# Four of seven products of the mixer's sets with high and low parts side by side

## The chip, the cores and the metric

One core of a Trainium2 chip runs one launch of the kernel. The metric is the device time in microseconds (us), the median of the runs shown. All times below are in us unless ns is said.

## The reference, cut to what matters

The block is two gated feed-forward networks (FFNs) with a mixer between them; everything is float32, with 512 tokens and a width of 1024.

```python
x = x + 0.5 * swiglu(rmsnorm(x, g1), w_gu1, w_down1)      # 1024 -> 2 x 2816 -> 1024
h = rmsnorm(x, gm)
z = h @ w_in                                              # 1024 -> 8208 columns
cb, cc, cu, q, k, v, g_lr, r, ga, gb = split(z)
y_conv = (cb * causal_short_conv(cc * cu, conv_w)) @ w_out_conv
o = gla_chunked(q, k, v, log_a)                           # gated linear attention, 4 heads, chunks of 64
y_gla = (norm(o) * silu(r)) @ w_out_gla
x = x + (sigmoid(ga) * y_conv + sigmoid(gb) * y_gla) @ w_o
x = x + 0.5 * swiglu(rmsnorm(x, g2), w_gu2, w_down2)
return rmsnorm(x, gf)
```

## The kernel before, in words

**Products.** TensorE multiplies in fp32r. To keep float32's precision each operand is split in two: a high part (the value rounded to fp32r) and a low part (the rest). A product is then three passes: high weights on high data, high weights on low data, low weights on high data. ScalarE makes a weight's high part (`wh`, line 346), VectorE its low part (`wl`, line 347); three buffers of each exist, and `Weights.issue` makes the parts of step n+2 when step n is taken.

**Sets.** Most large matrices are multiplied in *sets*: a 2 by 2 grid of blocks is multiplied with seven block products in place of eight (Winograd's form of Strassen's scheme). The seven are called m1, p2, q6, p5, q7, p4, p3. One block product takes 512 rows of the matrix and 256 of its columns (in two halves e = 0, 1 of 128) on 256 tokens, so a pass is 4 k-blocks times 2 halves = 8 matmuls. The products share accumulators: "b" is written by m1, q6, q7 and p4, one on top of the other; "c" by p5 and then p3; "a" by p2. So after m1, q6 and q7 the state of "b" has to be copied out before the next of them may be written, and the quarters of the result are made from these copies with sums: p2's quarter is a + m1; q7's, made after q7 from p5's c, is -c - (copy at q7); p3's is c + (copy at q6); p4's is -b. Sets are numbered 0 to 11 (on `w_in`) and 12, 13 (on `w_out_gla`). `order` fixes the order of products: q6, p5, q7 of set s, m1 of the next set t, p4 of s, p2 of t, p3 of s. The last set ends q6, p5, q7, p2, p4, p3, and the first begins m1, p2.

**Two kinds of sets.** The FFNs' up sets (`PairSet`, line 562) have tiles of two PSUM banks. For most of them (`merged`) the high and low data lie side by side (`Both`, line 537: 256 high and 256 low columns per k-block), and high weights run over both in one matmul of 512 columns: left half of the tile is weights on high data, right half weights on low data; the low weights then add on the left half. That is 8 matmuls of 512 and 8 of 256. Left and right are added later by ScalarE and VectorE (`taken`, `onto`, `whole`). The mixer's sets (`Set`, line 494) use one bank per accumulator and 24 matmuls of 256 columns a product (line 517): 12 sets on `w_in` (`MSETS`: ga, gb, ga, conv, gb, conv, conv, conv, cb, cb, r, r) and 2 on `w_out_gla`. From the second set on a set is `forked`: after m1 ScalarE copies bank b into bank a (line 522), and p2 accumulates on that copy; after q6 and q7 ScalarE copies bank b to an SBUF tile of the pool `tp` (line 525).

**Around the sets.** `run_sets` (line 762) runs the products in order and calls hooks between them: the attention's steps (`gates`, `decays`, `scale`, `scores`, `state`, `output`, `squares`) for the four heads are hung on products of the first nine sets. `conv_done`, `cb_done`, `gate_done`, `r_done` and `gla_done` use the quarters: products with each other and a three-tap convolution (`convolve`, lines 1393 to 1396), gates stored to DRAM from the ScalarE queue (line 1481), silu, or the final sum (line 1600). Statements further down, such as the split of the convolution's result (`split_pair`, lines 1513 and 1514), get their place in each engine's queue from the compiler's own schedule, so they can run between products. After the `w_out_gla` sets the product with `w_o` starts with a group of four accumulators (`mm_group`, line 395).

**PSUM.** There are 8 banks. `banks` opens either six single banks (pool `mm`) and two more (pool `aux`, used by hooks and norms), or, for the up sets, four pairs with the names w, x, y, z. The pools lie one behind another in the order in which they are opened; a newly opened `mm` pool hands out its places in the order 0, 5, 4, 3, 2, 1 (this is how the program before is laid out), and later the place that has been free longest. The last plain product before FFN 1's up sets leaves its accumulator in bank 0, and w, the first pair, lies on banks 0 and 1.

Of the kernel before, what the change touches and what calls it, by code (L numbers as in the profile page):

```python
# [8 lines left out]
F32 = mybir.dt.float32  # L9
F32R = mybir.dt.float32r  # L10
# [169 lines left out]
def block_kernel(ctx: ExitStack, tc: tile.TileContext, xT, vecs, gf, gup, wgl, wts, out):  # L180
# [23 lines left out]
    def T(dtype=F32):  # L204
        return tile_of("tp", [P, S], dtype)

    stage = ExitStack()

    def banks(paired=False):

        stage.close()
        for n, b in (("pairs", 1),) if paired else (("mm", 6), ("aux", 2)):
            cnt[0] += 1
            pools[n] = stage.enter_context(tc.tile_pool(
                name=f"{n}{cnt[0]}", bufs=b, space=bass.MemoryType.PSUM, reuse_waits="tile"))

    banks()
    ctx.push(lambda *_: stage.close())
# [274 lines left out]

    class Set:


        def __init__(self, group_, done):
            self.group = group_
            self.done = done
            self.bank = {}  # L500
            self.v = {}

        def run(self, p):
            b = {"m1": "b", "p2": "a", "q6": "b", "p5": "c", "q7": "b", "p4": "b", "p3": "c"}[p]
            fresh = b not in self.bank
            if fresh:
                self.bank[b] = MM()
            o = self.bank[b]
            bh, bl = self.group.get(p)
            h, l = W.take()  # L510
            for j, (ww, aa) in enumerate(((h, bh), (h, bl), (l, bh))):
                for k in range(4):
                    for e in range(2):
                        s = slice(k * HW + e * P, k * HW + (e + 1) * P)
                        t = slice(k * HW, (k + 1) * HW)
                        to = o[:, e * HW : (e + 1) * HW]
                        nc.tensor.matmul(to, ww[:, s], aa[:, t],  # L517
                                         start=fresh and k == 0 and e == 0 and j == 0,
                                         stop=k == 3 and j == 2, skip_group_check=True)
            if p == "m1" and self.forked:  # L520
                self.bank["a"] = MM()
                nc.scalar.copy(self.bank["a"], o)  # L522
            elif p in ("m1", "q6", "q7"):
                v = T()
                nc.scalar.copy(v, o)
                self.v[p] = v
            self.done(self, p)

        def first(self):

            if self.forked:
                return self.bank["a"]
            t = T()
            nc.vector.tensor_tensor(out=t, in0=self.bank["a"], in1=self.v["m1"], op=ALU.add)
            return t
# [26 lines left out]
    class PairSet:  # L562
# [21 lines left out]
        def run(self, p):  # L584
# [4 lines left out]
            h, l = W.take()  # L589
            first = fresh  # L590

            def product(to, ww, aa):
                nonlocal first
                for k in range(4):
                    for e in range(2):
                        nc.tensor.matmul(to(e), ww[:, k * HW + e * P : k * HW + (e + 1) * P],  # L596
                                         aa(k), start=first and k == 0 and (self.merged or e == 0),
                                         stop=k == 3 and ww is l, skip_group_check=True)
                first = False

            if self.merged:
                product(lambda e: o[:, e], h, x_.both)
                product(lambda e: o[:, e, :HW], l, x_.high)
            else:
                half = self.flat(n)
                for ww, aa in ((h, x_.high), (h, x_.low), (l, x_.high)):
                    product(lambda e: half[:, e * HW : (e + 1) * HW], ww, aa)
# [41 lines left out]

    class Operands:  # L650
# [5 lines left out]
        def __init__(self, b, kind=None):  # L656
            self.b = b
            self.kind = kind
# [22 lines left out]
        def make(self, p):  # L681
# [6 lines left out]
            if self.kind is not None:  # L688
                self.parts[p] = self.kind(v)
                return  # L690
            h, l = (tile_of("op", [P, 1024], F32R) for _ in range(2))
            hv, lv = (t.rearrange("p (k t) -> p k t", t=HW) for t in (h, l))
            nc.scalar.copy(hv, v)
            nc.vector.tensor_tensor(out=lv, in0=v, in1=hv.bitcast(F32), op=ALU.subtract)
            self.parts[p] = (h, l)
# [4 lines left out]
    class DownOperands:  # L700
# [17 lines left out]
        def make(self, p):  # L718
# [11 lines left out]
            h, l = (tile_of("op", [P, 1024], F32R) for _ in range(2))  # L730
            hv, lv = (t.rearrange("p (k t) -> p k t", t=HW) for t in (h, l))
            nc.scalar.copy(hv, v)
            nc.vector.tensor_tensor(out=lv, in0=v, in1=hv.bitcast(F32), op=ALU.subtract)
            self.parts[p] = (h, l)
# [4 lines left out]
    def natural_set(ops, bank, done, ahead=1):  # L739

        used = {"a"}
        for at, p in enumerate(SEQ):
# [6 lines left out]
            bh, bl = ops.get(p)  # L749
            for u in range(2):  # L750
                h, l = W.take()
                for j, (ww, aa) in enumerate(((h, bh), (h, bl), (l, bh))):
                    for i in range(2):
                        k = 2 * u + i
                        for t in range(2):
                            s = slice(k * HW + t * P, k * HW + (t + 1) * P)
                            nc.tensor.matmul(o[t], aa[:, s], ww[:, i * 512 : (i + 1) * 512],  # L757
# [932 lines left out]
```

## Time and profile before

| | before |
|---|---|
| median of 3 runs | 1174.29 (1173.33 to 1174.67) |
| profiled execution: its time, its span | 1173.69, 1172.0 |
| granted TensorE clock, mean | 0.999 |
| the mixer's first 12 sets and the hooks between them | about 430 to 703 |
| the two `w_out_gla` sets | about 747 to 787 |
| FFN up sets | about 51 to 228 and 876 to 1056 |

The page gives busy time, share of the span and number of instructions of each engine, the chain of work that ended last, and the costliest groups of instructions. PE is TensorE, PEld its weight load, DVE VectorE, ACT ScalarE. Other views are the waits (who waited for whom), the timeline (instructions in order of start: start, duration, engine, line, operation, out<-in, and idle time before it in brackets), groups by line, and windows (busy time of each engine in a stretch). Ends of matmuls are modelled and overlap; the pace of TensorE is read from the starts.

### The profile page before, as it was taken

Reading aid. Unit: us, or ns where it says so; the run is one execution under the profiler, and the core shown is the slowest. Engines: PE = TensorE matmul, PEld = TensorE weight load, DVE = VectorE, ACT = ScalarE, POOL = GpSimd, SP = SyncE. Lnnn points to the kernel's source line nnn. Section 1 sums busy time; section 2 is a strip of 40 time slices with the busy share of each in tenths; the row PEclk is TensorE's granted clock in tenths of the full one; section 3 lists DMA queues with packets and bytes.
Section 4 is the critical chain, followed back from the end, with each engine's and each line's share of the span. In section 5 each row is a group of like instructions: output and inputs, shape, how many; then the busy total and the mean of one; then the engine's idle time right before and its main releaser. Section 6 shows DMA issues by size and latency. Waiting matters only on the chain.

```text
span 1172.0 us, 17786 instructions
## 1 busy us (share of the span) xinstructions
PE 1163.1 (99%) x7010; PEld 1038.9 (89%) x7010; DVE 922.0 (79%) x1125; ACT 668.5 (57%) x860; POOL 117.1 (10%) x153
## 2 busy tenths in 40 slices
PE   9999999999999999999999999999999999999997
PEld 8898888988888889999999998998889888898886
DVE  7997888996578965767697788586599788889955
ACT  6576666675335655565565476544456666666443
POOL 0010101111010111100111100000001111011100
PEclk9999999999999999999999999999999999999999
DMA  9477787778524488777687766540638777767721
GB/s 352 85 203 197 175 203 180 164 192 218 199 90 109 93 206 225 187 179 200 177 204 189 205 187 198 130 125 22 239 75 213 178 191 178 192 153 186 181 84 72
DMA packets 62596, 200.16 MB, mean 171 GB/s; under 512 B 6864, under 2 KB 13136, under 8 KB 62512
## 3 DMA queue, kind: packets, MB, share of 16 engines
q1 hardware_dynamic: 39088, 126.37, 32.4%
q0 software_dynamic: 18784, 68.17, 31.4%
q10 hardware_dynamic: 4640, 4.49, 1.1%
q8 instruction: 55, 0.90, 0.3%
q14 instruction: 29, 0.24, 0.1%
HBM read 124.55 MB, written 8.39 MB: 113 GB/s over the span
## 4 chain that ended last, share of the span: by engine, by line
PE 95%; DVE 2%; ACT 2%; issue 1%; ACTq 0%; POOL 0%; POOLq 0%
PE mm L517 22%; PE mm L757 13%; PE mm L381 9%; PE y L596 9%; PE w L596 9%; PE z L596 9%; PE mm L395 7%; PE x L596 4%; PE mm L974 4%; PE aux L757 4%; PE aux L974 1%; PE aux L1297 1%; PE aux L1278 1%; PE aux L1256 1%; DVE wl L347 0%
## 5 line engine op out<-in xcount | busy, mean ns | idle before, releaser
L346 ACT CAST wh<-f 128x1024 fp32r<-128x1024 f32 (+1 forms) x341 | 356.4, 1047 | 369.4 <-PE mm L517 86.2
L347 DVE TENSOR_TENSOR wl<-f,wh 128x1024 fp32r<-128x1024 f32 (+1 forms) x341 | 412.8, 1216 | 122.6 <-ACT wh L346 113.5
L517 PE MATMUL mm<-op,wh 128*128 128x256 f32 x1568 | 208.1, 285 | 0.4 <-ACT mm L522 0.4
L324 POOL DMA_DIRECT2D f<-f x126 | 108.6, 862 | 921.8 <-DVE wl L347 524.1
L517 PEld LDWEIGHTS mm<-op,wh 128*128 128x128 f32 x1568 | 196.9, 191 | 2.1 <-ACT mm L522 0.8
L517 PE MATMUL mm<-op,wl 128*128 128x256 f32 x784 | 110.0, 283 | 0.0
L757 PE MATMUL mm<-wh,op 128*128 128x512 f32 x432 | 106.9, 389 | 0.0
L517 PEld LDWEIGHTS mm<-op,wl 128*128 128x128 f32 x784 | 101.2, 192 | 0.1
L757 PEld LDWEIGHTS mm<-wh,op 128*128 128x128 f32 x432 | 80.9, 188 | 16.7
L381 PE MATMUL mm<-op,wh 128*128 128x512 f32 x384 | 91.0, 389 | 0.0
L381 PEld LDWEIGHTS mm<-op,wh 128*128 128x128 f32 x384 | 72.0, 188 | 15.0
L596 PE MATMUL w<-op,wh 128*128 128x512 f32 (+1 forms) x352 | 73.1, 353 | 0.5 <-DVE tp L491 0.5
L596 PE MATMUL y<-op,wh 128*128 128x512 f32 (+1 forms) x384 | 73.3, 338 | 0.0
L596 PE MATMUL z<-op,wh 128*128 128x512 f32 (+1 forms) x320 | 72.7, 371 | 0.0
L596 PEld LDWEIGHTS y<-op,wh 128*128 128x128 f32 x384 | 58.4, 190 | 6.2
L395 PE MATMUL mm<-op,wh 128*128 128x512 f32 x256 | 63.8, 391 | 0.0
L596 PEld LDWEIGHTS w<-op,wh 128*128 128x128 f32 x352 | 56.2, 190 | 8.2 <-issue 0.9
L596 PEld LDWEIGHTS z<-op,wh 128*128 128x128 f32 x320 | 54.0, 189 | 8.2
L757 PE MATMUL mm<-wl,op 128*128 128x512 f32 x216 | 57.7, 389 | 0.0
L395 PEld LDWEIGHTS mm<-op,wh 128*128 128x128 f32 x256 | 47.8, 188 | 10.3
L333 DVE TENSOR_TENSOR f<-f,f 128x1024 f32<-128x1024 f32 x42 | 51.3, 1221 | 0.8
L757 PEld LDWEIGHTS mm<-wl,op 128*128 128x128 f32 x216 | 40.5, 188 | 8.4
(313 smaller groups left out, 1690.4 us busy)
## 6 DMA issues: line engine op xcount, KB each, us to landing
f<-wts SPq DMA_DIRECT2D x219, 512.0 KB, 4.5
f<-f POOLq DMA_DIRECT2D x126, 512.0 KB, 5.0
X<-xT SPq DMA_DIRECT2D x8, 256.0 KB, 5.3
xs<-X POOLq DMA_DIRECT2D x8, 256.0 KB, 2.4
ga<-tp ACTq DMA_DIRECT2D x8, 256.0 KB, 3.2
gb<-tp ACTq DMA_DIRECT2D x8, 256.0 KB, 3.7
tp<-ga SPq DMA_DIRECT2D x8, 256.0 KB, 4.2
y<-tp SPq DMA_DIRECT2D x7, 256.0 KB, 2.3
```

The costliest lines, as they stand in the source:

```text
L324: return nc.gpsimd.dma_start(out_, a, accum_op=ALU.add).ins
L333: nc.vector.tensor_tensor(out=s3, in0=a11, in1=a21, op=ALU.add)
L346: self.cast = nc.scalar.copy(h[:, :w], raw[:, :w]).ins
L347: nc.vector.tensor_tensor(out=l[:, :w], in0=raw[:, :w], in1=h[:, :w].bitcast(F32), op=ALU.subtract)
L381: nc.tensor.matmul(o, w[:, i * P : (i + 1) * P], a[k], start=j == k == 0, stop=j == 2 and k == kt - 1)
L395: nc.tensor.matmul(o[c], w[:, s : s + P], a[k], start=k == 0 and j == 0, stop=k == kt - 1 and j == 2)
L517: nc.tensor.matmul(to, ww[:, s], aa[:, t], start=fresh and k == 0 and e == 0 and j == 0, stop=k == 3 and j == 2, skip_group_check=True)
L596: nc.tensor.matmul(to(e), ww[:, k * HW + e * P : k * HW + (e + 1) * P], aa(k), start=first and k == 0 and (self.merged or e == 0), stop=k ...
L757: nc.tensor.matmul(o[t], aa[:, s], ww[:, i * 512 : (i + 1) * 512], start=fresh and j == k == 0, stop=j == 2 and k == 3, skip_group_check=True)
L974: nc.tensor.matmul(o[t][e], b if j == 1 else a, wl if j == 2 else wh, start=k == K0 and e == 1 and j == 0, stop=k == KF - 1 and j == 2, sk ...
L1256: nc.tensor.matmul(st[:, b], k_[:, b], q_[:, b], start=True, stop=True)
L1278: nc.tensor.matmul(kv[:, hc], E[:, t * P : (t + 1) * P], v[t][:, (h % 2) * DV : (h % 2) * DV + DV], start=True, stop=True)
```

## The change

The mixer's sets get the FFN's form for the four products that write "b" (m1, q6, q7, p4); p2, p5 and p3 keep their 24 matmuls of 256 columns. `xo` and the `w_out_gla` operands become `Both` tiles (two casts and two subtractions of 512 elements where there was one of 1024 each). While sets run, PSUM holds `aux` (2 banks), two pairs of banks with the name bb, and two single banks; `aux` is opened first and stays open, so singles and pairs lie behind it. The fork is gone: after m1 the two halves of bb are added to an SBUF tile (`sum`: one ScalarE copy of the right half, one VectorE addition of the left), and p2 starts on a bank of its own; after q6 and q7 two ScalarE copies and one VectorE addition take the place of one copy; p2's and p4's quarters take an addition that they did not need. The scratch tiles of pool `tp` get names: m0, m1, q0, q1 for values that are kept, s0 and s1 by turns for the rest while sets run, all six by turns elsewhere; q7's copy goes to the norm's `acc` tile. For the up sets the four pairs are opened in the order w, x, z, y, and w now lies where `aux` was.

```diff
+    def banks(kind="plain"):
+        want = {"plain": ((("aux", 2),), (("mm", 6),)),
+                "pairs": ((), (("pairs", 1),)),
+                "mixed": ((("aux", 2),), (("pairs", 2), ("mm", 2)))}[kind]
...
+        if kind == "pairs":
+            for tag in "wxzy":
+                MM2(tag)
...
+        def wide(self, o):
+            for w, a, n in ((self.h, self.x.both, 2 * HW), (self.l, self.x.high, HW)):
+                for k in range(4):
+                    for e in range(2):
+                        nc.tensor.matmul(o[:, e, :n],
+                                         w[:, k * HW + e * P : k * HW + (e + 1) * P], a(k),
...
     class Set:
...
-                self.bank[b] = MM()
+                self.bank[b] = MM2("bb") if b == "b" else MM()
...
-            if p == "m1" and self.forked:
-                self.bank["a"] = MM()
-                nc.scalar.copy(self.bank["a"], o)
-            elif p in ("m1", "q6", "q7"):
-                v = T()
-                nc.scalar.copy(v, o)
-                self.v[p] = v
+            product = Product(*W.take(), x_, fresh)
+            if b != "b":
+                product.narrow(o)
+            else:
+                product.wide(o)
+                if p != "p4":
...
+                    if p == "m1":
+                        self.sum(v)
+                    else:
+                        r = T()
+                        nc.scalar.copy(pair(v), o[:, :, :HW])
+                        nc.scalar.copy(pair(r), o[:, :, HW:])
+                        nc.vector.tensor_tensor(out=v, in0=v, in1=r, op=ALU.add)
...
+        def sum(self, t):
+            o = self.bank["b"]
+            nc.scalar.copy(pair(t), o[:, :, HW:])
+            nc.vector.tensor_tensor(out=pair(t), in0=o[:, :, :HW], in1=pair(t), op=ALU.add)
+            return t
+
+        def quarter(self, p):
+            if p == "p4":
+                return self.sum(T())
+            b, n = {"p2": ("a", "m1"), "q7": ("c", "q7"), "p3": ("c", "q6")}[p]
+            t = self.v[n]
+            if p == "q7":
+                nc.vector.scalar_tensor_tensor(out=t, in0=self.bank[b], scalar=-1.0, in1=t,
+                                               op0=ALU.mult, op1=ALU.subtract)
+            else:
+                nc.vector.tensor_tensor(out=t, in0=self.bank[b], in1=t, op=ALU.add)
+            return t
...
             def done(s, p):
-                bank, v = s.bank, s.v
                 u = Y[i][:, :, 2:]
                 if p == "p2":
-                    s.t1 = s.first()
-                    if s.forked:
-                        s.t1 = T()
-                        nc.scalar.copy(s.t1, bank["a"])
+                    s.t1 = s.quarter(p)
...
+        narrow_ring()
+        banks("mixed")
         run_sets(make, hooks=hooks)
         finish_late()
+        banks()
+        wide_ring()
...
-        run_sets(lambda i: Set(oo, gla_done(i)), hooks={(0, "p3"): [reload]})
+        narrow_ring()
+        banks("mixed")
+        run_sets(lambda i: Set(oo, gla_done(i), i), hooks={(0, "p3"): [reload]})
         finish_late()
+        banks()
+        wide_ring()
```

More of the change, by code (lines that the diff above doesn't have):

```diff
@@ L520, in run @@
-            if p == "m1" and self.forked:
-                self.bank["a"] = MM()
-                nc.scalar.copy(self.bank["a"], o)
-            elif p in ("m1", "q6", "q7"):
-                v = T()
-                nc.scalar.copy(v, o)
-                self.v[p] = v
-            self.done(self, p)
[L529 to L534, printed above, removed]
+            x_ = self.group.get(p)
@@ L588, in run @@
             x_ = self.group.get(p)
[L589 to L599, printed above, removed]
+            product = Product(*W.take(), x_, fresh)
             if self.merged:
-                product(lambda e: o[:, e], h, x_.both)
-                product(lambda e: o[:, e, :HW], l, x_.high)
-            else:
-                half = self.flat(n)
-                for ww, aa in ((h, x_.high), (h, x_.low), (l, x_.high)):
-                    product(lambda e: half[:, e * HW : (e + 1) * HW], ww, aa)
+                product.wide(o)
+            else:
+                product.narrow(self.flat(n))
             if p == "m1" and self.forked:
@@ L687, in make @@
             v = self.sum(p)
[L688 to L695, printed above, removed]
+            self.parts[p] = Both(v)
         def get(self, p):
@@ L729, in make @@
                     "p3": (1, 1), "p4": (1, 0)}[p])
[L730 to L734, printed above, removed]
+            self.parts[p] = Apart(v)
         def get(self, p):
```

169 lines of the change are left out of this document (88 added, 81 removed).

## The prediction

> **What bounds the kernel now.** I read the page first, for the engines' shares and the chain of work that ended last.
>
> ```profile
> span 1172.0 us, 17786 instructions
> ...
> PE 1163.1 (99%) x7010; PEld 1038.9 (89%) x7010; DVE 922.0 (79%) x1125; ACT 668.5 (57%) x860; POOL 117.1 (10%) x153
> ...
> PE mm L517 22%; PE mm L757 13%; PE mm L381 9%; PE y L596 9%; PE w L596 9%; PE z L596 9%; PE mm L395 7%; PE x L596 4%; PE mm L974 4%; PE aux L757 4%; PE aux L974 1%; PE aux L1297 1%; PE aux L1278 1%; PE aux L1256 1%; DVE wl L347 0%
> ```
>
> TensorE is on the chain nearly throughout, and the line that the change rewrites, L517, holds 22% of it. So what counts is how many ns each product takes on TensorE, and whether TensorE has to wait for another engine. The second view is the list of waits, TensorE's own:
>
> ```profile
> PE aux L239 <- POOL ones L236: 1.1, 1, 1.1
> PE w L596 <- DVE tp L491: 0.5, 1, 0.5
> PE mm L517 <- ACT mm L522: 0.4, 2, 0.2
> ```
>
> Three kinds of wait, 2.0 us in all. Nothing feeds TensorE late today; the change can gain on pace and lose on new waits. The third view is the pace. First wide products in an FFN's up sets, then narrow ones in a mixer set, both from the timeline of TensorE:
>
> ```profile
> 95.95 2.00 PE L596 MATMUL y<-op,wh 128*128 128x512 f32 x8
> 97.79 1.12 PE L596 MATMUL y<-op,wl 128*128 128x256 f32 x8
> 98.74 2.00 PE L596 MATMUL z<-op,wh 128*128 128x512 f32 x8
> ```
>
> ```profile
> 642.83 2.08 PE L517 MATMUL mm<-op,wh 128*128 128x256 f32 x16
> 644.75 1.12 PE L517 MATMUL mm<-op,wl 128*128 128x256 f32 x8
> 645.71 2.08 PE L517 MATMUL mm<-op,wh 128*128 128x256 f32 x16
> ```
>
> From start to start a wide product takes 98.74 - 95.95 = 2.79 us, a narrow one 645.71 - 642.83 = 2.88 us. The difference is in the high weights: eight matmuls of 512 take 1.84 us, sixteen of 256 take 1.92. The fourth view is a table of stretches, for VectorE (third pair of numbers) and ScalarE (fourth):
>
> ```profile
> core 0: us, PE busy (x) PEld busy (x) DVE busy (x) ACT busy (x) POOL busy (x), PEclk, DMA share, GB/s
> 94.00:226.00 132.00, 132.00 (x807) 118.38 (x806) 110.79 (x124) 83.49 (x108) 15.39 (x19) 1.00 0.74 184
> 430.00:683.00 253.00, 252.61 (x2051) 247.83 (x2051) 179.78 (x228) 145.15 (x192) 27.87 (x35) 1.00 0.75 192
> 524.00:544.00 20.00, 20.00 (x169) 20.00 (x168) 19.93 (x28) 13.16 (x19) 1.72 (x2) 1.00 0.64 167
> 578.00:602.00 24.00, 23.77 (x194) 23.37 (x194) 22.54 (x34) 17.85 (x25) 2.58 (x3) 1.00 0.56 148
> 781.00:791.70 10.70, 10.70 (x72) 9.80 (x71) 10.66 (x14) 4.56 (x5) 0.00 (x0) 1.00 0.17 49
> ```
>
> The first row is the FFN's wide sets: VectorE is 84% busy and TensorE never stops. Over the mixer's sets (second row) VectorE is busy 71% of the time. But the last three rows are stretches in which it is full: 19.93 of 20.00, 22.54 of 24.00, 10.66 of 10.70. There it has no room for anything, and the change gives it more to do.
>
> **The change, part by part.**
>
> *Pace.* Four products of seven in 14 sets turn wide: 56 products x (2.88 - 2.79) us = 5.0 us. This lies wholly on the path. The other 42 products stay at 2.88: their rows have the same columns, and the data only lie in another tile.
>
> The Trainium skill ("TensorE: Matmul & The Clock Gate", section "Back-to-back issue gap") gives a warm matmul N/2.4 + 2.5 ns, 109 ns at 256 columns and 216 at 512; by that, as an estimate, a product goes from 2.62 to 2.60 us and all 56 save 1.1 us. The trace does not agree: its matmuls take 120 and 230 ns, and the wide product saves four times as much.
>
> *Waits that go.* The two ScalarE forks before p2 (0.4 us) go, since p2 now starts on a bank of its own. The wait of w at FFN 1's first up set (0.5 us) goes: w no longer lies on bank 0, which the last plain product's VectorE evacuation still holds. What is late next there is x at p2, 2.8 us later, by which time both evacuations are over. Together 0.9. FFN 2's start has no such wait and gains nothing.
>
> *What is added on the other engines.* Per set VectorE gets five additions of 128x512 (after m1, q6, q7, in p2's and p4's quarters); ScalarE gets two or three more copies. Their price:
>
> ```profile
> L1456 DVE TENSOR_TENSOR tp<-mm,tp 128x512 f32<-128x512 f32 x9 | 6.2, 685 | 5.6 <-PE mm L517 5.6
> ```
>
> ```profile
> L525 ACT COPY tp<-mm 128x512 f32<-128x512 f32 x30 | 17.5, 584 | 0.0
> ```
>
> So 5 x 0.685 = 3.4 us of VectorE and 1.2 to 1.8 us of ScalarE a set. Over 430 to 683 (11 sets) VectorE goes from 180 to 180 + 38 = 218 of 253: still room on average, and the cover is the lead of `wl`, which is made up to three products ahead. Where that lead is short the additions cost. Splitting the operands in halves adds one short ScalarE and one short VectorE instruction per operand, 14 operands, before and between the products; the FFN's row shows the same work hidden, so nothing.
>
> *Place 1, the stretch 578 to 602.* The low weights of q6 in set 7:
>
> ```profile
> 599.69 2.35 DVE L347 TENSOR_TENSOR wl<-f,wh 128x1024 fp32r<-128x1024 f32 x2
> 602.05 0.52 PE L517 MATMUL mm<-op,wl 128*128 128x256 f32 x3
> ```
>
> The first of the two subtractions is over near 600.9, and TensorE uses it at 602.05: a lead of 1.15 us, the shortest in the sets behind set 0. Between 578 and here VectorE gets five more additions, 3.4 us, into a full queue, and TensorE arrives 0.35 us sooner (four wide products). Bare, that is a stall of 2.6 us. The lower bound is 0, if the additions are queued where VectorE waits anyway (1.46 us of the 24) and later work moves back. That the queue is not in the order of the program is seen at 682.58, where a subtraction of line 1514, far behind the sets, runs between two products:
>
> ```profile
> 682.58 1.23 DVE L1514 TENSOR_TENSOR op<-y,op 128x1024 fp32r<-128x1024 f32 x1 [0.17 <-ACT op L1513]
> ```
>
> I take 1.6. The stretch before it, 524 to 544, ends with a lead of 3.0 us:
>
> ```profile
> 542.84 1.22 DVE L347 TENSOR_TENSOR wl<-f,wh 128x1024 fp32r<-128x1024 f32 x1
> 547.06 0.52 PE L517 MATMUL mm<-op,wl 128*128 128x256 f32 x3
> ```
>
> 3.0 - 3.4 - 0.35 makes 0 to 0.8; I take 0.3.
>
> *Place 2, set 0.* q6 writes b again one product after m1, and now waits for a copy and an addition:
>
> ```profile
> 434.24 2.36 DVE L347 TENSOR_TENSOR wl<-f,wh 128x1024 fp32r<-128x1024 f32 x2 [5.54 <-ACT wh L346]
> ...
> 435.06 0.58 ACT L525 COPY tp<-mm 128x512 f32<-128x512 f32 x1
> ...
> 435.69 1.98 PEld L517 LDWEIGHTS mm<-op,wh 128*128 128x128 f32 x16 [0.17 <-ACT tp L525]
> ```
>
> Today TensorE goes on right behind the copy, at 435.69. The addition starts at the copy's end, or at 436.6 behind both subtractions: 0.7 or 1.6 us later. I take 0.8, because an evacuation stands ahead of the second subtraction in the program. In later sets two or three products lie between m1 and q6, and the wait is covered; only set 12 begins as set 0 does, without the late weights, and I bound it by 0 and 0.7 and take 0.
>
> *Place 3, q7 before p4.* Two copies must be over in the one product between; twice TensorE already starts p4 on the heels of the single copy:
>
> ```profile
> 472.35 0.57 ACT L525 COPY tp<-mm 128x512 f32<-128x512 f32 x1
> ...
> 472.97 0.38 PE L517 MATMUL mm<-op,wh 128*128 128x256 f32 x1
> ```
>
> ```profile
> 781.51 0.66 PEld L517 LDWEIGHTS mm<-op,wh 128*128 128x128 f32 x5 [0.15 <-ACT tp L525]
> ```
>
> A second copy costs 0.58 each, 1.2 for both, 1.8 if ScalarE is late by one more copy; 0.6 if one of them finds its engine free. I take 0.8.
>
> *Place 4, the start of `w_o`.* While sets run there are two single banks; behind the last set a new `mm` pool opens, and its first four places hold both of them and two of the pairs' banks. So the group of four at L395 has the bank of p3, set 13, as its second or third accumulator, and waits for its evacuation:
>
> ```profile
> 787.37 2.00 PE L395 MATMUL mm<-op,wh 128*128 128x512 f32 x8
> 788.15 0.68 DVE L1600 TENSOR_TENSOR y<-y,g 128x512 f32<-128x512 f32 x1
> 788.75 0.68 DVE L1456 TENSOR_TENSOR tp<-mm,tp 128x512 f32<-128x512 f32 x1
> ```
>
> Before, that evacuation (L1456) ended at 789.43 and nobody waited. Now the third matmul, at 787.37 + 2 x 0.23 = 787.83, would: 1.6 us. Three additions of set 13 (q7, p2, p4) stand ahead of it in a queue that is full from 781 on, so up to 1.6 + 2.05 = 3.6; the lower bound is an addition right behind the product, 0.4. I take 1.6, the lateness that the row shows. The Trainium skill ("Perfetto Trace Analysis", section "Matmuls") says that independent matmul groups should rotate through different PSUM banks so that evacuation overlaps the next group; by that rule this place must cost, and the trace agrees at the one place where it was broken before, w's 0.5 us.
>
> *Sum.* Gain 5.0 + 0.9 = 5.9; loss 1.6 + 0.3 + 0.8 + 0.8 + 1.6 = 5.1; net -0.8. The profiled execution took 1173.69 around its span of 1172.0 and comes to 1172.9; the median of the runs is 0.6 above it, so I forecast 1173.5 for the median, 0.07% less. A measurement of this kernel can tell about 0.2%, 2.35 us, from no change.
>
> **The rivals.**
>
> *The additions find room.* VectorE's queue is rewritten by the schedule, all four places come out at their lower bounds: 0 + 0 + 0.7 + 0.6 + 0.4 = 1.7, net -4.2, 1170.1. For it: the FFN's wide sets run at 84% VectorE without a stall, and the mixer's average after the change is 86%. Against it: the full stretches, where work cannot move earlier.
>
> *VectorE becomes the bound in the full stretches.* Place 1 at 2.6 + 0.8, place 2 at 1.6 + 0.7, place 4 at 3.6, place 3 as taken, 0.8: 10.1, net +4.2, 1178.5. It decides as soon as more than 1.15 us, two additions, are queued ahead of the low weights of set 7's q6. For it: 22.54 of 24.00 and 10.66 of 10.70. Against it: TensorE gets no wait from any low weights today, even where VectorE is full.
>
> *The wide product saves less than it does in the FFN*, and the change does not do what it says: at a saving of 0.02 us a product (1.1 in all) and the same losses the net is +3.1, 1177.4. Against it: two wide products in the rows above, one after the other, at 2.79. (This is the matmul page's formula.)
>
> **How the numbers follow.** Forecast 0.40, room for the additions 0.35, VectorE the bound 0.22, less saved 0.03. The forecast's own terms stay within 2.35 us of before, the first rival lies beyond on the fast side, the other two on the slow side: faster 0.35, same 0.40, slower 0.25. The range reaches from the first rival's 1170.1, less 0.7 for m1's evacuation in set 0 if it is hidden, to the second's: 1169.4 to 1178.5.
>
> **What would show it.** The steps are right if m1, q6, q7 and p4 take 2.79 us from start to start in the mixer; if w at FFN 1 and the mixer's p2 have no wait; and if the list of TensorE's waits has new rows: low weights from VectorE near set 7's q6, an addition after m1 in set 0, a ScalarE copy before p4 in sets 1 and 13, and VectorE before the group at `w_o`. The forecast is wrong if those rows add up to under 2.5 or over 7.5 us, or if p2, p5 and p3 take other than 2.88. If VectorE shows idle time in front of `wl` waiting for ScalarE in the stretches above, it was not full, and the first rival holds.

## The result and the profile after

| | before | after |
|---|---|---|
| median of 6 runs each | 1174.43 (1173.33 to 1174.71) | 1181.16 (1180.42 to 1182.26) |
| ratio, 95% interval | | 1.0060 (1.0047 to 1.0073) |
| profiled execution: span, granted clock | 1172.0, 0.999 | 1179.0, 0.996 |

The kernel became 0.6% slower. The forecast was 1173.5, its range ended at 1178.5: both wrong. The engines' shares after (page, part 1):

```profile
PE 1161.8 (99%) x6562; PEld 1016.6 (86%) x6562; DVE 962.9 (82%) x1207; ACT 686.7 (58%) x909; POOL 117.2 (10%) x153
```

VectorE went from 79% to 82%, as the additions say; that row doesn't show 7 us. The list of TensorE's waits does:

```profile
PE mm L418 <- DVE tp L594: 4.7, 1, 4.7
PE bb L537 <- DVE tp L581: 2.5, 2, 1.5
...
PE mm L806 <- DVE wl L370: 0.8, 1, 0.8
PE bb L537 <- DVE wl L370: 0.4, 1, 0.4
```

The waits of before on `w` and on the ScalarE fork are gone. In their place TensorE waits 4.7 us once at the group of four of `w_o` (L418), for the evacuation of p3 of set 13 (L594); twice, 2.5 us in all, behind m1 of sets 0 and 12 for its addition (L581); and 0.8 us in the set of v (L806). With the 0.4 of the last row that makes 8.4 us, and the span grew by 7.0 in spite of the gain in pace. Where the rest is, TensorE's timeline shows at the first of these places:

```profile
785.54 1.12 PE L528 MATMUL mm<-op,wl 128*128 128x256 f32 x8
786.50 0.63 PE L418 MATMUL mm<-op,wh 128*128 128x512 f32 x2
791.86 2.93 PE L418 MATMUL mm<-op,wh 128*128 128x512 f32 x6 [4.73 <-DVE tp L594]
794.58 1.91 PE L418 MATMUL mm<-op,wl 128*128 128x512 f32 x4
796.29 2.48 PE L418 MATMUL mm<-op,wh 128*128 128x512 f32 x8
```

Two matmuls of the group run, the third stands until 791.86. Then look at the starts: four matmuls take 796.29 - 794.58 = 1.71 us, 427 ns each, where a matmul of 512 columns takes about 230 elsewhere. TensorE's clock had been halved while it stood: in this trace the granted clock is 0.50 from 790.5 to 797.3. From the group's start to the start of the next product it is 815.86 - 786.50 = 29.4 us, and before 809.16 - 787.37 = 21.8: 7.6 us lost here, 4.9 by the wait and 2.7 by the clock. All the rest of the kernel together is 0.6 us faster than before.

VectorE was not full at that place. The windows, of the stretches that the prediction used:

```profile
core 0: us, PE busy (x) PEld busy (x) DVE busy (x) ACT busy (x) POOL busy (x), PEclk, DMA share, GB/s
431.00:683.00 252.00, 250.00 (x1704) 229.80 (x1703) 210.88 (x282) 158.22 (x218) 27.84 (x35) 1.00 0.75 194
578.00:602.00 24.00, 24.00 (x162) 22.00 (x160) 22.28 (x35) 18.30 (x26) 1.72 (x2) 1.00 0.55 144
781.00:791.70 10.70, 5.90 (x40) 5.02 (x38) 8.20 (x11) 4.84 (x6) 0.00 (x0) 0.94 0.26 71
```

From 781 to 791.7 VectorE is busy 8.20 us, before it was 10.66; it has more to do and does less. The granted clock is 0.94 there. VectorE's timeline shows the hole, and what stood behind it:

```profile
780.22 0.69 DVE L1624 SCALAR_TENSOR_TENSOR g<-acc,g 128x512 f32<-128x512 f32 x1
783.50 1.23 DVE L370 TENSOR_TENSOR wl<-f,wh 128x1024 fp32r<-128x1024 f32 x1 [2.59 <-ACT wh L369]
784.64 0.68 DVE L1628 TENSOR_TENSOR y<-y,g 128x512 f32<-128x512 f32 x1
785.25 0.68 DVE L594 TENSOR_TENSOR tp<-mm,tp 128x512 f32<-128x512 f32 x1
785.85 1.21 DVE L370 TENSOR_TENSOR wl<-f,wh 128x1024 fp32r<-128x1024 f32 x1
...
789.38 1.22 DVE L370 TENSOR_TENSOR wl<-f,wh 128x1024 fp32r<-128x1024 f32 x1
790.52 0.68 DVE L1628 TENSOR_TENSOR y<-y,g 128x512 f32<-128x512 f32 x1
791.12 0.68 DVE L594 TENSOR_TENSOR tp<-mm,tp 128x512 f32<-128x512 f32 x1
```

VectorE stands 2.59 us in front of the low weights of p3, then works without a pause through eleven instructions, and the evacuation that TensorE needs is the last of them. ("If VectorE shows idle time in front of `wl` ...", the prediction said, "it was not full"; that has come true.) The low weights waited for the high ones, and those for a DMA that adds one block of weights to another (f to f, from GpSimd's queue). Its issue before and after, ScalarE's cast before and after:

```profile
775.08 0.86 POOL L324 DMA_DIRECT2D f<-f  x1 [16.76 <-DVE wl L347]
...
779.93 1.05 ACT L346 CAST wh<-f 128x1024 fp32r<-128x1024 f32 x1 [2.99 <-DMA f<-f]
```

```profile
776.09 0.86 POOL L347 DMA_DIRECT2D f<-f  x1 [18.47 <-ACT op L1543]
...
782.42 2.95 ACT L369 CAST wh<-f 128x1024 fp32r<-128x1024 f32 x3 [3.69 <-DMA f<-f]
```

The DMA was issued 1.0 us later and took 6.2 us to land in place of 4.7, so the cast ran 2.5 us later, while TensorE came to that product 1 us sooner. By the program the DMA overwrites the block from which the low weights of p2 are made; these started at 774.35 in place of 773.56, now behind an addition. The view puts the DMA's start down to ScalarE's cast of line 1543, over 0.1 us before it; which of the two held it is open.

The hole is not new. Before the change it lay 2.5 us earlier:

```profile
781.01 1.23 DVE L347 TENSOR_TENSOR wl<-f,wh 128x1024 fp32r<-128x1024 f32 x1 [2.63 <-ACT wh L346]
```

The window from 781 begins just behind it. From these low weights to the evacuation it was 788.75 - 781.01 = 7.74 us before and is 791.12 - 783.50 = 7.62 after, so the additions did not make this stretch longer. Before, the evacuation ended 1.6 us behind the place where the third matmul now needs the bank; it now starts 2.4 us later and the group 0.9 us sooner, together the 4.9 us.

### The profile page after: what moved, and what is told of

Same layout as the page of the kernel before. It is cut to its first block, busy times and chain, and to the rows that moved or that the text cites. A ratio compares the mean times of both kernels' runs of the same rounds, so it can differ in the third digit from the quotient of the medians.

```text
span 1179.0 us, 17042 instructions
## 1 busy us (share of the span) xinstructions
PE 1161.8 (99%) x6562; PEld 1016.6 (86%) x6562; DVE 962.9 (82%) x1207; ACT 686.7 (58%) x909; POOL 117.2 (10%) x153
## 4 chain that ended last, share of the span: by engine, by line
PE 57%; DVE 3%; DMA 1%; ACT 1%; issue 1%; DVEq 0%; ACTq 0%
PE bb L537 11%; PE mm L528 8%; PE mm L404 7%; PE mm L806 5%; PE mm L418 4%; PE z L537 4%; PE w L537 3%; PE y L537 3%; PE mm L1023 2%; PE x L537 2%; PE aux L806 2%; PE y L528 1%; DMA f<-f 1%; DVE wl L370 1%; PE w L528 1%; PE aux L1023 1%
## 5 line engine op out<-in xcount | busy, mean ns | idle before, releaser
L537 PE MATMUL bb<-op,wh 128*128 128x512 f32 x448 | 114.3, 396 | 2.5 <-DVE tp L581 2.5
L806 PE MATMUL mm<-wh,op 128*128 128x512 f32 x432 | 106.9, 389 | 0.0
L537 PEld LDWEIGHTS bb<-op,wh 128*128 128x128 f32 x448 | 81.0, 189 | 18.0 <-DVE tp L581 2.9
L806 PEld LDWEIGHTS mm<-wh,op 128*128 128x128 f32 x432 | 80.9, 188 | 16.7
L528 PE MATMUL mm<-op,wh 128*128 128x256 f32 x672 | 88.6, 284 | 0.2 <-ACT wh L369 0.2
L404 PEld LDWEIGHTS mm<-op,wh 128*128 128x128 f32 x384 | 72.0, 188 | 15.0
L528 PEld LDWEIGHTS mm<-op,wh 128*128 128x128 f32 x672 | 84.0, 191 | 0.8 <-ACT wh L369 0.4
L418 PE MATMUL mm<-op,wh 128*128 128x512 f32 x256 | 66.0, 400 | 4.7 <-DVE tp L594 4.7
L537 PEld LDWEIGHTS bb<-op,wl 128*128 128x128 f32 x448 | 61.0, 190 | 5.0 <-DVE wl L370 0.6
L537 PE MATMUL z<-op,wh 128*128 128x512 f32 x256 | 64.4, 393 | 0.0
L537 PE MATMUL bb<-op,wl 128*128 128x256 f32 x448 | 62.5, 282 | 0.4 <-DVE wl L370 0.4
L418 PEld LDWEIGHTS mm<-op,wh 128*128 128x128 f32 x256 | 48.8, 193 | 16.2 <-DVE tp L594 5.2
L806 PE MATMUL mm<-wl,op 128*128 128x512 f32 x216 | 57.9, 390 | 0.8 <-DVE wl L370 0.8
L537 PE MATMUL w<-op,wh 128*128 128x512 f32 x224 | 56.3, 393 | 0.0
L537 PEld LDWEIGHTS z<-op,wh 128*128 128x128 f32 x256 | 46.0, 189 | 8.2
L806 PEld LDWEIGHTS mm<-wl,op 128*128 128x128 f32 x216 | 40.5, 188 | 9.6 <-DVE wl L370 1.3
L537 PE MATMUL y<-op,wh 128*128 128x512 f32 x192 | 48.3, 393 | 0.0
```

What stands on the lines that cost most here:

```text
L404: nc.tensor.matmul(o, w[:, i * P : (i + 1) * P], a[k], start=j == k == 0, stop=j == 2 and k == kt - 1)
L418: nc.tensor.matmul(o[c], w[:, s : s + P], a[k], start=k == 0 and j == 0, stop=k == kt - 1 and j == 2)
L528: nc.tensor.matmul(o[:, e * HW : (e + 1) * HW], w[:, k * HW + e * P : k * HW + (e + 1) * P], a(k), start=self.fresh and j == k == e == 0, ...
L537: nc.tensor.matmul(o[:, e, :n], w[:, k * HW + e * P : k * HW + (e + 1) * P], a(k), start=self.fresh and k == 0 and w is self.h, stop=k == ...
L806: nc.tensor.matmul(o[t], a(k)[:, t * P : (t + 1) * P], ww[:, i * 512 : (i + 1) * 512], start=fresh and j == k == 0, stop=j == 2 and k == 3 ...
```

## Experiments

Theory: one bank (p3 of set 13 holds the third accumulator of `w_o`'s group), VectorE's late arrival at it, and the clock that falls meanwhile make 7.5 us; the rest are single waits. Rival: VectorE is the bound, and TensorE would stop somewhere else. Medians of before lay at 1174.45, 1174.18 and 1174.56 in the three series, each on one chip.

### Free banks for the group

```diff
-        o = [MM() for _ in cols]
+        o = [AUX() if c < aux else MM() for c in range(len(cols))]
...
+mm_group("w_o", KD, (0, P, 2 * P, 3 * P), m_h, m_l, aux=2)
```

> The changed kernel, with one edit: the first two of the four accumulators of the group at w_o come from the aux pool, whose two banks lie idle there, and only the other two from the new mm pool; so none of the four is the bank that p3 of set 13 still holds. Theory T (the bank): the time that the changed kernel lost, 4.7 us of waiting and some 2.7 us in which 512-column matmuls took 427 ns each, hangs on this one bank; without it the wait at the group is under 0.3 us, the group takes 21.8 us again as before the change (29.4 now), and the run comes to 1181.2 - 7.5 = 1173.7 us. Rival R (VectorE is the bound): the third accumulator is only where TensorE happens to stop; VectorE is 5 us behind, so the low weights or the operands of the next products come late instead, TensorE stops a little further on, and the time stays above 1178.

Measured: 1173.75 (1172.62 to 1175.65), ratio to before 0.9998 (0.9989 to 1.0007). The wait is gone and the group runs at full pace:

```profile
785.51 1.12 PE L528 MATMUL mm<-op,wl 128*128 128x256 f32 x8
786.48 1.09 PE L418 MATMUL aux<-op,wh 128*128 128x512 f32 x4
787.40 0.62 PE L418 MATMUL aux<-op,wl 128*128 128x512 f32 x2
```

VectorE's queue is as late as before: the same evacuation starts at 791.11. Nobody waits for it now. So the lateness did harm through that bank alone: the theory holds, the rival falls.

### The wait filled with unread matmuls

```diff
+[nc.tensor.matmul(q, w[:, s : s + P], a[k], start=True, stop=True) for q in fill_ if k == j == 0 and c == 1]
...
+mm_group("w_o", KD, (0, P, 2 * P, 3 * P), m_h, m_l, fill_=[AUX()] * 20)
```

> The changed kernel, with 20 matmuls of 512 columns more behind the first two matmuls of the group at w_o; their results go to an idle bank and are never read. They take 20 x 0.23 = 4.6 us, about as long as TensorE stands idle there, and take no wait away. Theory T (the idle lowers the clock): what follows the wait at 427 ns a matmul does so because TensorE stood idle; kept busy it goes on at about 230 ns, the matmuls behind the wait save about 2.65 us, and the run comes to 1178.5 us, with the evacuation ending when it did. Rival R (contention or late data, not idleness, slows those matmuls): they stay at over 400 ns and the time stays at 1181 us.

Measured: 1178.45 (1177.70 to 1179.01).

```profile
790.50 1.29 PE L419 MATMUL aux<-op,wh 128*128 128x512 f32 x5
791.99 1.66 PE L418 MATMUL mm<-op,wh 128*128 128x512 f32 x6 [0.20 <-DVE tp L594]
793.49 1.07 PE L418 MATMUL mm<-op,wl 128*128 128x512 f32 x4
794.39 1.98 PE L418 MATMUL mm<-op,wh 128*128 128x512 f32 x8
```

The evacuation comes no sooner (791.99, after: 791.86), but the matmuls behind it run at full speed, the first six in 1.50 us where they took 2.72. Doing more work made the kernel 2.7 us faster: that is the price of the clock, apart from that of the wait.

### The same bank, freed by ScalarE

```diff
-                nc.vector.tensor_tensor(out=t, in0=self.bank[b], in1=t, op=ALU.add)
+                nc.vector.tensor_tensor(out=t, in0=self.copied(self.bank[b]) if p == "p3" and self.last else self.bank[b], in1=t, op=ALU.add)
...
+        def copied(self, o):
+            c = T(); nc.scalar.copy(c, o); return c
```

> The changed kernel, with one ScalarE copy more: the last product of the last set (p3 of set 13) is copied out of its bank by ScalarE right behind the product, and VectorE adds from the copy. The banks are handed out as in the changed kernel, and VectorE's queue has the same entries in the same order. Theory T (the bank's release is late, VectorE's lateness itself harms nobody): the wait shrinks from 4.7 us to about 0.5 us, the clock stays up, and the run comes to about 1181.2 - 7.5 + 0.5 = 1174.2 us. Rival R (VectorE is the bound): the queue is as late as before and TensorE stops later for its low weights, so the time stays above 1178.

Measured: 1175.07 (1173.64 to 1177.79), ratio 1.0006 (0.9997 to 1.0015). Two short waits are left at the group, 0.5 us for the addition of p4 and 0.2 for the new copy. A second way to free the bank wins back 6.1 of the 7.4 us; what VectorE's lateness itself costs at the group is the 0.5 us, through the bank of p4.

### Part undone: sets 12 and 13 narrow again

```diff
-        narrow_ring()
-        banks("mixed")
-        run_sets(lambda i: Set(oo, gla_done(i), i), hooks={(0, "p3"): [reload]})
+        run_sets(lambda i: NarrowSet(oo, gla_done(i), i), hooks={(0, "p3"): [reload]})
```

(`NarrowSet`: one bank of the plain pool per accumulator, `narrow` for all seven, the fork and single copies as before.)

> Part of the change undone: sets 12 and 13 (out of GLA) go back to seven narrow products in one bank each of the plain pool, with the ScalarE fork, as before the change; the twelve sets on w_in keep the wide form. Then no pool is changed in front of w_o. Theory T: the group at w_o takes 21.8 us again, the stall behind m1 of set 12 (1.2 us) goes, 8 wide products cost 8 x 0.09 = 0.7 us more, and the gain of the twelve sets (3.4 us from the start of set 0 to the end of the sets on w_in, less 1.7 us of later start) is what is left: 1173.0 us, below the kernel before by 1 to 2 us. Rival R (the change loses time all over, through the additions): still above 1176.

Measured: 1174.00 (1172.09 to 1175.18), ratio 0.9995 (0.9986 to 1.0004), 1.0 above what was expected. Nearly the whole loss lies in the last two sets and what follows them. The twelve sets on `w_in` by themselves give no gain clear of the noise in this form (0.4 us); the wait behind m1 of set 0 (1.3 us) and that in the set of v (0.8) are still in its list.

### Without the DMA that p3 waited for

```diff
-            if p == "p2":
+            if p == "p2" and (self.early, at) != (4, max(i for i in range(self.end) if STEPS[i][1] == "p2")):
                 self.add(a12, a11)
```

> The changed kernel, without the one DMA that adds one block of weights to another (f to f, on GpSimd's queue) for p3 of set 13; that product then runs on the plain block, so a sum of the computation is left out. The banks are handed out as in the changed kernel. Theory D (head of the line): VectorE reached the evacuation that TensorE waited for late because its queue stood 2.6 us (780.9 to 783.5) behind the low weights of that product, whose cast waited for this DMA, with work ready behind them; the additions alone make the rest of the 4.7 us. Then the wait falls to about 2.1 us, the clock stays up, so the slow matmuls (2.65 us) go too, and the run comes to 1181.2 - 2.6 - 2.65 = 1176 us. Rival A (the additions alone fill the queue, and the DMA is hidden): the wait stays over 4 us and the time at 1181.

Measured: 1175.81 (1173.40 to 1176.85). The banks still collide, and the wait is 1.0 us in place of 4.7, with full clock behind it:

```profile
788.54 0.63 PE L418 MATMUL mm<-op,wh 128*128 128x512 f32 x2
790.19 1.67 PE L418 MATMUL mm<-op,wh 128*128 128x512 f32 x6 [1.02 <-DVE tp L594]
791.70 1.09 PE L418 MATMUL mm<-op,wl 128*128 128x512 f32 x4
```

This kernel leaves out one sum, so it only prices the wait. Theory D holds, more strongly than it was put: without the DMA 1.0 of the wait is left, the blocked queue made 3.7. Why the transfer took 6.2 us to land and not 4.7 was not tried.

### m1 of the first sets on left halves

```diff
-                product.wide(o)
+                product.left(o) if p == "m1" and not self.forked else product.wide(o)
...
-                        self.sum(v)
+                        self.sum(v) if self.forked else nc.scalar.copy(pair(v), o[:, :, :HW])
```

(`left`: the 24 matmuls of `narrow`, onto `o[:, e, :HW]`; on top of the free banks.)

> The version with free banks at w_o, with m1 of the first set of each of the two runs (sets 0 and 12) as 24 matmuls of 256 columns all onto the left halves of its pair of banks, evacuated by one ScalarE copy as before the change; the other products as in the change. Theory T: the two waits for the addition behind m1 (1.6 and 1.2 us, 2.7 in the list of waits) go, two products cost 0.09 us more each: 1173.75 - 2.5 = 1171.2 us. Rival R (VectorE is the bound, the waits only move): the low weights come late a product later and the time stays at 1173 or above.

Measured: 1170.54 (1170.35 to 1170.97), ratio 0.9967 (0.9954 to 0.9979): faster than before. TensorE's waits:

```profile
PE aux L262 <- POOL ones L259: 1.1, 1, 1.1
PE mm L806 <- DVE wl L370: 0.8, 1, 0.8
PE bb L537 <- DVE wl L370: 0.4, 1, 0.4
PE mm L528 <- ACT wh L369: 0.3, 1, 0.3
PE bb L537 <- ACT tp L569: 0.3, 1, 0.3
```

3.2 us gained, 2.5 expected, and the runs now lie within 0.6 us of each other, not within 3. The run without the DMA shows why: in its profiled execution the wait behind m1 of set 0 also halved the clock. Its row, then that of the same place in the run of the next experiment:

```profile
439.94 3.27 PE L537 MATMUL bb<-op,wh 128*128 128x512 f32 x8 [2.11 <-DVE tp L581]
443.00 1.56 PE L537 MATMUL bb<-op,wl 128*128 128x256 f32 x8
```

```profile
438.58 2.11 PE L537 MATMUL bb<-op,wh 128*128 128x512 f32 x8 [2.26 <-DVE tp L581]
```

Eight matmuls took 3.06 us from start to start in the one, and about 1.95 in the other, whose wait was the longer (the last section has a reason). In the runs with free banks alone a mean clock of 0.997 goes with 1175.4 to 1175.7, 0.998 with 1173.2 to 1175.6, and 0.999 with 1172.6 to 1174.6. That it is this place in every one of those runs is likely, but not shown: only one execution of each kernel is profiled.

### An operand made later

```diff
                 if c == QO and h == 2:
                     xo.make("m1")
...
+                elif c == KO: xo.make("p2")
```

> The version with free banks at w_o, with the making of one operand (p2 of the first operands on w_in) moved in the program from before to behind the last k product of head 3, so that the low weights of the second half of m1 in the set of v stand ahead of the operand's norms and halves in VectorE's queue. Theory T: the wait of 0.8 us in front of L806 (393.90), where TensorE stopped 0.99 us longer than its pace, goes, and nothing else changes: 1172.8 us. Rival R (the operand itself comes late instead, with p2 of v): no gain, 1173.7 or above.

Measured: 1174.38 (1172.54 to 1176.78), ratio 1.0000 (0.9991 to 1.0009); no gain. But the wait in front of L806 is gone:

```profile
PE bb L537 <- DVE tp L581: 3.3, 2, 2.3
PE aux L262 <- POOL ones L259: 1.1, 1, 1.1
PE mm L418 <- DVE op L451: 0.5, 1, 0.5
```

The wait behind m1 of set 0 is 2.3 us here (after: 1.5; with free banks: 1.7). Neither theory as it was put: the operand doesn't come late, and still the time isn't gained. It looks as if the wait moved to the next place at which TensorE needs VectorE; the first run of the last series is to show it.

### Four of the additions left out

```diff
-                        nc.scalar.copy(pair(r), o[:, :, HW:])
-                        nc.vector.tensor_tensor(out=v, in0=v, in1=r, op=ALU.add)
...
-            nc.scalar.copy(pair(t), o[:, :, HW:])
-            nc.vector.tensor_tensor(out=pair(t), in0=o[:, :, :HW], in1=pair(t), op=ALU.add)
+            nc.scalar.copy(pair(t), o[:, :, :HW])
```

> The version with free banks at w_o, with the right halves left out: m1, q6, q7 and p4 are evacuated from the left half by one ScalarE copy each, so that the products of the high weights with the low parts are computed by TensorE but never added; four of the five additions per set and one copy of two go. It prices the additions as a whole: what is left is the pace of the wide products. Theory T (the additions cost only at the places named): the waits behind m1 of sets 0 and 12 go, 2.7 us, and some 0.5 us before p3 of set 13: 1170.5 us. Rival R (the additions cost all over the sets, by many small stops): 1168.5 or less, the time before less the whole gain of 5.9.

Measured: 1170.16 (1169.51 to 1171.21), ratio 0.9966 (0.9954 to 0.9978). This kernel leaves out part of the product, so it only prices the additions. The version with m1 on left halves takes 0.4 us more and does 54 of the 56 additions that are left out here; over 431 to 683 VectorE is busy 188 us in this run and 211 with free banks alone. This run's profile has a wait that that one's hasn't, 0.8 us at L1373 (the next section shows it in another run), so the additions may be worth 1.2 us. Where TensorE doesn't wait for them at once they cost little: theory T holds and the rival falls.

### All three mended, and the clock by idle time

The last series: the three edits together; then, on the changed kernel with m1 on left halves as the only edit (the bank still in the way), 0, 5 and 10 unread matmuls ahead of the group.

> Free banks at w_o, m1 of sets 0 and 12 on left halves, and the operand made behind the last k product of head 3, all three together. Theory M (a wait that moved): with free banks alone the third edit took the 0.8 us in front of L806 away and the wait behind m1 of set 0 grew from 1.7 to 2.3 us in its place; where that wait is gone the whole 0.8 to 1.0 us is gained: 1170.54 - 0.9 = 1169.6 us. Rival R (something else feeds TensorE 1 us late there whatever is mended): 1170.5, no gain.

> The changed kernel with m1 of sets 0 and 12 on left halves as its only edit; the four accumulators of the group at w_o come from the new mm pool as in the change, bank of p3 included. If the losses are separate and add up (theory T): 2.7 us of waits go, with the half clock that in some runs follows the wait in set 0, and the 7.5 us at w_o stay: 1178.2 us. Rival S (one backlog carried from set to set, so that mending the first waits also shortens the last): 1175 or less.

> The version before in this list (changed kernel, m1 on left halves) with 5 unread matmuls of 512 columns more ahead of the group at w_o: TensorE is idle for about 4.7 - 5 x 0.23 = 3.6 us in place of 4.7, and the end of the wait stays where it was. Theory I (the clock falls behind any idle time of some 2 us and more): the matmuls behind the wait still take 427 ns, for about as long as before, and the time is that of the version without the fill, 1178. Rival J (the clock falls only behind 4 us or more): full speed behind the wait, 1175.5.

> As the run with 5 unread matmuls, with 10: idle for about 2.4 us. Profiles so far had half clock behind an idle time of 2.11 us in set 0 once and full clock behind 2.26 us once, so about 2.1 to 2.3 us is where it starts. Theory I: both outcomes are seen among the runs of this kernel, some near 1178 (clock fell) and some near 1175.5 (it didn't). Rival J: all near 1175.5.

| edit | median | runs |
|---|---|---|
| all three | 1169.87 | 1169.39 to 1170.05, and one 1174.14 |
| m1 left, bank in the way | 1178.15 | 1177.35 to 1178.87 |
| the same, 5 unread matmuls | 1177.61 | 1176.56 to 1179.75 |
| the same, 10 unread matmuls | 1177.70 | 1177.01 to 1179.54 |

All three together make 0.9958 of before (0.9944 to 0.9971), the best version here, 4.7 us faster. With m1 mended the operand's edit gains 0.7 us where it gained nothing alone, and four of its five runs lie below all five of the version without it; the two ratios' intervals overlap, so theory M fits and is not shown beyond doubt. The run of 1174.14 is the profiled one, and has a wait that only the run without the additions shares (0.8 us there), VectorE's for a scratch tile that a store of gates still read (TensorE's wait for it, then VectorE's row):

```profile
PE aux L1373 <- DVE tp L428: 2.6, 1, 2.6
```

```profile
464.01 0.69 DVE L428 TENSOR_TENSOR tp<-g,tp 128x512 fp32r<-128x512 f32 x1 [2.70 <-DMA ga<-tp]
```

While sets run only two scratch tiles go round (s0, s1). The clock fell behind this wait too: its 2.6 us and the 1.7 that 3.4 us of half clock cost make up the 4.3 us by which this run lies above the median. How often that happens is open.

The losses add up: the bank costs 1178.15 - 1170.54 = 7.6 us with m1 mended, and 1181.16 - 1173.75 = 7.4 without. Rival S falls. The fills, idle 3.6 and 2.4 us:

```profile
789.41 2.20 PE L418 MATMUL mm<-op,wh 128*128 128x512 f32 x6 [3.59 <-DVE tp L594]
791.41 1.91 PE L418 MATMUL mm<-op,wl 128*128 128x512 f32 x4
```

```profile
789.40 2.93 PE L418 MATMUL mm<-op,wh 128*128 128x512 f32 x6 [2.45 <-DVE tp L594]
792.12 1.22 PE L418 MATMUL mm<-op,wl 128*128 128x512 f32 x4
```

Both still fall to half clock (four matmuls in 1.71 us from start to start in the first; six in 2.72 in the second), so rival J falls. The mixture that theory I expected with 10 can't be read from the times, since four of those seven runs spent 2.9 to 3.5 us outside the span from first to last instruction, where most runs spend 1.7 to 2.0. The medians of the spans alone are 1176.4, 1175.8 and 1175.2 with 0, 5 and 10. By the granted clock the mixture is there, once: one of the seven has 0.999; profiles without a fall have 0.998 or 0.999, those with one 0.996 or 0.997. It is not a profiled run, and its span, 1174.7, is only 0.5 below the median, so that stays open.

## Why the prediction was wrong

The step that failed is place 4, the start of `w_o`: 1.6 us in the sum, 0.4 to 3.6 in its bounds, 7.6 measured. The place and the bank were named rightly, and so was the direction. By the prediction's own sign, new rows of over 7.5 us in the list of waits (8.4 here), it was wrong. Two things were missing. First, the upper bound counted instructions, "Three additions of set 13 (q7, p2, p4) stand ahead of it in a queue that is full from 781 on". Before the change the queue was full from 781 on because VectorE had stood for 2.6 us just ahead of that, behind an instruction that waited for a DMA. The change moved this wait 2.5 us later and brought TensorE to the group 0.9 us sooner; the sum allowed for neither, and the additions that it did count made the stretch no longer (7.62 us, 7.74 before). Without the DMA the third matmul starts 790.19 - 788.54 - 0.45 = 1.2 us late, close to the 1.6 taken. Second, the sum had no term for the clock: idle time was charged at its own length, and the 4.7 us here cost 2.7 more. With this place mended the kernel takes 1173.75, within 0.3 of the forecast, but by luck: the other terms miss in both directions. The other steps:

- *Pace*, 5.0: right. Two wide products in the mixer start 639.25 - 636.46 = 2.79 us apart, in the timeline after:

```profile
636.46 2.00 PE L537 MATMUL bb<-op,wh 128*128 128x512 f32 x8
638.30 1.11 PE L537 MATMUL bb<-op,wl 128*128 128x256 f32 x8
639.25 2.00 PE L537 MATMUL bb<-op,wh 128*128 128x512 f32 x8
```

- *Waits that go*, 0.9: right, both rows are gone.
- *Operands in halves*, "hidden, so nothing": wrong in the set of v. Halves are ready sooner, and two of them got ahead of low weights in VectorE's queue: 1.0 us of delay, and taking it away gave nothing until m1 was mended.
- *Place 1*, 1.6 and 0.3: 0.4 (the last row of the waits) and nothing. The schedule moved work; VectorE was busy 22.28 of the 24.00 us there, no more than before.
- *Place 2*, 0.8 for set 0 and 0 for set 12: 1.6, its upper bound, and 1.2, above the bound of 0.7. Set 12 does begin as set 0 does.
- *Place 3*, 0.8: 0.2. Neither of the two places named has a wait. At a third one p4's weight load (PEld) waits for the second copy, and its first matmul starts 0.2 us late:

```profile
542.71 1.70 PEld L537 LDWEIGHTS bb<-op,wh 128*128 128x128 f32 x8 [0.21 <-ACT tp L573]
```

Added up as measured, the losses are 7.6 + 1.0 + 0.4 + 1.6 + 1.2 + 0.2 = 12.0 us, and two waits of 0.2 and 0.3 stand elsewhere in the list; less the gain of 5.9 that is 6.6 of the 7.0 us by which the span grew.

The second rival, VectorE as the bound in full stretches, came nearest in time and is wrong as a mechanism: four additions a set more on VectorE cost 0.4 to 1.2 us, and the stretch that it was read from was full before and is not after. The first rival, room for the additions, is right of the sets and wrong of their end.

## What to carry to other kernels

When pools of PSUM banks are changed between two stages, look up which banks the next stage takes first, and give it those that have been free longest. For a late evacuation don't count only the instructions ahead of it: look among them for one that waits for a DMA, since what was ready behind it stood with it here, for 2.59 us. And ask whether the engine stood just ahead of a stretch that looks full: here that wait was in the trace before the change. A wait of TensorE of more than some 2 us may cost 1.5 to 2.7 us on top for the clock.

## What the runs showed of the hardware

After idle times of 2.45, 2.58, 3.59 and 4.73 us, in five profiles, TensorE ran 3 to 12 matmuls of 512 columns at 427 ns in place of 230; after 2.11 us too, after 2.07 and 2.26 us in two others not, after 1.0 to 1.7 us never. The half clock need not start at once: behind 3.59 us some matmuls still ran at full speed.

The traces' record of the granted clock shows why the length alone doesn't decide. It changes in steps of 3.413 us: half clock in mid-kernel lasted 3.41 us four times and 6.83 us twice, and the stretches at full clock are whole multiples too (785.065 us is 230 of them). So the borders of these steps can be laid through every profile, back from a change of the clock. The idle time within each step, and the clock behind:

| profile | idle, us | of it in the two steps that it touches | clock behind |
|---|---|---|---|
| the change | 4.73 | 3.35, 1.38 | half for 6.83 us |
| m1 left, bank in the way | 4.73 | 2.12, 2.61 | half for 6.83 us |
| the same, 5 unread matmuls | 3.59 | 1.07, 2.52 | half for 3.41 us |
| all three | 2.58 | 2.52, 0.06 | half for 3.41 us |
| m1 left, 10 unread matmuls | 2.45 | 2.01, 0.44 | half for 3.41 us |
| the operand made later | 2.26 | 1.50, 0.76 | full |
| without the DMA | 2.11 | 2.11 | half for 3.41 us |
| the wait filled | 2.07 | 1.10, 0.97 | full |

The clock fell behind each step with 2.0 us or more of idle time, and behind none at full clock with 1.5 or less. The ends of the 14 profiles, where TensorE stops, agree: it fell behind the first step with 2.2 us or more, and not behind those with 0.7 to 1.5. The price is half of the busy time at half clock: in the change (6.83 - 1.38) / 2 = 2.7 us, what the filled wait won.

The Trainium skill ("TensorE: Matmul & The Clock Gate", section "Why this matters for your kernels") asks for no idle gaps of over some 3 us between matmuls; here 2.11 was enough, and the measurement decides. The same page of the Trainium skill ("What's actually happening") has the clock set by a window of about 3.4 us that runs freely, so that the phase matters; these traces agree, with 3.413 us and the cases of 2.07, 2.11 and 2.26.
